# Grouped-query heads: softmax weights scaled on POOL ahead of their transposes, output kept feature-major

## The chip, the cores and the metric

The kernel runs on one core of one Trainium2 chip. The metric is device time in microseconds of one execution, lower is better. Engines: PE does the matrix products and the transposes, PEld loads its stationary operands, DVE (vector), ACT (scalar, activations) and POOL (the general engine) do the elementwise work, SP issues the DMAs. Each engine has its own queue and works through it in order.

## The reference

The reference is a two-layer encoder over 1024 tokens of 1024 features, in float32. The change lies in one part of the first layer, the grouped-query attention ("B" heads): 8 query heads of 64 features share 2 key/value heads.

```python
def gqa_attention(q, k, v):
    scale = HEAD_DIM ** -0.5
    def block(qb):                       # 128 queries at a time
        s = jnp.einsum('bqgrd,bkgd->bgrqk', qb, k).astype(jnp.float32) * scale
        pr = jax.nn.softmax(s, axis=-1).astype(v.dtype)
        return jnp.einsum('bgrqk,bkgd->bqgrd', pr, v)
    return from_blocks(lax.map(block, to_blocks(q)))
...
    b_o = gqa_attention(b_q, b_k, b_v)
    mix = jnp.concatenate([a_o.reshape(b, s, A_V), b_o.reshape(b, s, B_Q)], axis=-1)
    return mix @ w_out
```

The softmax divides by the sum of its row. Whether that is done to the weights ahead of the product with V, or to the product, is the same in exact arithmetic.

## The kernel before, in words

**Three-product precision.** A float32 operand of a matrix product is kept as two parts: `hi`, rounded to PE's fast format (fp32r), and `lo`, what is left. A product is then hi·hi + hi·lo + lo·hi. Making the parts costs one ACT instruction (`hi`, a rounding copy) and one DVE instruction (`lo`, a subtraction) each time. `H` is the operand of the projections: features in partitions, tokens along the free dimension ("feature-major").

**The even mixer** (method `even`) runs 96 items in one software pipeline, `its`: u = 0 to 3 are the differential heads (8 items each, one per block of 128 queries), u = 4 and 5 are the two key/value heads of the grouped-query part, with 32 items each: 8 query blocks `qt`, and 4 query heads j in each. So the grouped-query items are n = 32 to 95. The loop over n calls `step(n)`; a step works on several items at different ages, and this order, written out by hand, is also the order of each engine's queue:

- `qk(n)`: scores on PE (lines 964 and 969) into an `S` tile of PSUM (2 buffers), their negated maximum on DVE (line 972);
- `tr(n - 2)`: eight 128x128 transposes on PE (line 1007) of the weights `P`, into two `b` banks of PSUM (4 buffers, shared with everything else that PE writes), and the rounding copies to `pt` on ACT (line 1017);
- `exp(n)`: the exponential on ACT, 128x1024, with its row sum (line 981);
- `tr2(n - 2)`: the `lo` parts on DVE (line 1029);
- `combine(n)`: for odd j, the reciprocals of the two row sums of a pair of heads (line 996);
- `pv(n - 3)`: for odd j, the product of both heads' `pt` with V, 16 matmuls (line 1044). V's `hi` sits in output partitions 0 to 63 and its `lo` in 64 to 127, so the result has two halves that still have to be added;
- `tail_b(n - 4)`: for odd j, two transposes of 64 rows (line 1073), and the multiplication by the reciprocals on DVE (line 1078), into a token-major tile `MS`;
- `tail_a(n - 3)`: for odd j, the addition of the two halves: a copy on ACT (line 1061), an addition on DVE (line 1062);
- `place_b(n - 5)`: once per query block, two 128x128 transposes of `MS` (line 1090), and the parts for `H` (lines 1093 and 1094);
- `background(2)`: two pieces of the rotary work of the key/value head that comes next, on POOL (lines 834 to 850). The last batch, 18 pieces, is queued at n = 37 and taken at 37 to 45.

Between the halves of a step the loop puts other work for PE: a tile of the input projection at steps up to 37 (lines 175 to 177, 384 columns), the transposes of `finish(5)` at 49 to 60, `place_a` (the differential heads' output, line 1090 on `mix`) at the even steps 40 to 54, and a tile of the output projection (512 columns) at steps 57 to 63 by 2 and 67 to 100 by 3.

`own` in the code names the two halves of the partitions: `own[0]` is 0 to 63, `own[1]` is 64 to 127. `self.os()` gives a small SBUF tile of 128x256 (7 buffers), `self.tb()` a PSUM bank `b`, `self.col()` a few columns for per-row values.

Of the kernel before, what the change touches and what calls it, by code (L numbers as in the profile page):

```python
# [11 lines left out]
F32 = mybir.dt.float32  # L12
F32R = mybir.dt.float32r
AF = mybir.ActivationFunctionType
ALU = mybir.AluOpType
# [10 lines left out]
P = 128  # L26
# [80 lines left out]
class Kern:  # L107
# [657 lines left out]
    def even(self, W, ready, load, after):  # L765
        nc, a = self.nc, self.a
# [25 lines left out]
        own = (slice(0, 64), slice(64, 128))  # L792
# [155 lines left out]
        L, MS = {}, {}  # L948
# [35 lines left out]
        def combine(n):  # L984
            u, qt, j = its[n]
            e = L[n]
            if u < 4:
                r = e["r"] = self.col(3)
                s0 = e["s"][:, 0:1]
                nc.vector.reciprocal(r[:, 0:2], e["s"])  # L990
                nc.vector.scalar_tensor_tensor(r[:, 2:3], s0, nlam, r[:, 1:2], op0=ALU.mult, op1=ALU.mult)
                nc.vector.scalar_tensor_tensor(e["P"][0], e["P"][1], r[:, 2:3], e["P"][0],
                                               op0=ALU.mult, op1=ALU.add)
            elif j % 2 == 1:
                r = e["r"] = self.col(2)
                nc.vector.reciprocal(r, e["s"])

        def tr(n):
            u, qt, j = its[n]
# [49 lines left out]
        def tail_a(n):  # L1049
            u, qt, j = its[n]  # L1050
            e = L[n]
            if u < 4:
                os = e["os"] = self.os()
                ss = self.col()
                xo = M[u][:, qt, :]
                nc.scalar.activation(os[:, :P], e["o"][:, :P], AF.Copy, scale=e["r"][:, 0:1])
                nc.scalar.activation(xo, os[:, :P], AF.Square, accum_out=ss)
                e["rs"] = self.rstd(ss, 1.0 / P)
            elif j % 2 == 1:
                os = e["os"] = self.os()  # L1060
                nc.scalar.copy(os[0:64], e["o"][64:128, :256])
                nc.vector.tensor_add(os[0:64], e["o"][0:64, :256], os[0:64])

        def tail_b(n):
            u, qt, j = its[n]
            e = L[n]
            if u < 4:
                xo = M[u][:, qt, :]
                nc.vector.scalar_tensor_tensor(xo, e["os"][:, :P], e["rs"], gs, op0=ALU.mult, op1=ALU.mult)
            elif j % 2 == 1:  # L1070
                ps = self.tb()
                for b in range(2):
                    nc.tensor.transpose(ps[:, b * 64:b * 64 + 64], e["os"][0:64, b * P:(b + 1) * P],
                                        self.ident[0:64, 0:64])
                if j == 1:
                    MS[u, qt] = self.os()
                xo = MS[u, qt][:, (j // 2) * P:(j // 2 + 1) * P].rearrange("p (h d) -> p h d", h=2)
                nc.vector.tensor_mul(xo, ps[:, :P].rearrange("p (h d) -> p h d", h=2),
                                     e["r"][:, :, None].to_broadcast([P, 2, 64]))
            L.pop(n)  # L1080

        its = [(u, qt, j) for u in range(6) for qt in range(NT) for j in range(1 if u < 4 else 4)]
# [2 lines left out]
        def place(src, k0, t):  # L1085

            ps = self.tb()
            n = len(src)
            for k, x in enumerate(src):
                nc.tensor.transpose(ps[:, k * P:(k + 1) * P], x, self.ident)  # L1090
            v = ps[:, :n * P].rearrange("p (k c) -> p k c", k=n)
            h, l = self.hT2(slice(k0, k0 + n), slice(t * P, (t + 1) * P))
            nc.scalar.copy(h, v)
            nc.vector.tensor_sub(l, v, h.bitcast(F32))
# [6 lines left out]
        def place_b(n):  # L1101
            u, qt, j = its[n]
            ms = MS.pop((u, qt))
            place([ms[:, :P], ms[:, P:]], 2 * u - 4, qt)

        def step(n):

            A = lambda m: 0 <= m < 32
            B = lambda m: 32 <= m < N
            if n < N:  # L1110
                qk(n)
            if A(n - 2):
                pv(n - 2)
            if B(n - 2):
                tr(n - 2)
            if n < N:
                exp(n)
            if B(n - 2):
                tr2(n - 2)
            if A(n - 2):  # L1120
                tail_a(n - 2)
            if A(n - 4):
                tail_b(n - 4)
            yield
            if A(n - 1):
                tr(n - 1)
                tr2(n - 1)
            if n < N:
                combine(n)
            if B(n - 3):  # L1130
                pv(n - 3)
            if B(n - 4):
                tail_b(n - 4)
            if B(n - 3):
                tail_a(n - 3)
            if B(n - 5) and its[n - 5][2] == 3:
                place_b(n - 5)
            background(4 if n < 32 else 2)
            yield
# [35 lines left out]
        for n in range(N + 6):  # L1175
# [4 lines left out]
            s = step(n)  # L1180
# [511 lines left out]
```

## Time and profile before

| | |
|---|---|
| median of 3 runs | 2802.2 us (2801.87 to 2803.43) |
| the profiled execution | 2802.09 us, span 2800.0 us |
| PE busy | 2735.4 us, 98% of the span |
| PEld | 2265.7 us, 81% |
| DVE | 1920.9 us, 69% |
| ACT | 1402.5 us, 50% |
| POOL | 669.5 us, 24% |
| mean granted TensorE clock | 0.992 of full speed |
| grouped-query stage | about 384 to 658 us |

The span is the profiled stretch of that execution, from the first to the last instruction. The busy share of an engine is an average over stages with different limits; what a change in one stage is worth is read from that stage. Matmuls are pipelined, so rows of PE overlap: a row's duration is longer than what it adds, and the distance between the starts of neighbours tells more. In brackets behind a row of the timeline stands the time the engine was idle ahead of it, and which instruction ended that.

### The profile page before, as it was taken

The numbers are of one execution on the slowest core, as the hardware profiler recorded it, in microseconds if no ns is written. First come the engines' busy times: TensorE is split into PE (matmuls) and PEld (weight loads), VectorE is DVE, ScalarE is ACT, GpSimd is POOL, SyncE is SP. The second block draws the span as 40 slices with busy tenths as digits, with TensorE's granted clock in tenths as the row PEclk, the third lists the DMA queues.
The fourth block names the chain that finished last, engine by engine and source line by source line (L and its number), as shares of the span: only waits on it lengthen the run. The fifth ranks groups of instructions, "written<-read, shape, count | busy, mean of one in ns | idle before, by whom it ended". The sixth has DMA issues, their size and how long they took to land. (4 is left out here: it accounts for less than half of the span.)

```text
span 2800.0 us, 37183 instructions
## 1 busy us (share of the span) xinstructions
PE 2735.4 (98%) x13776; PEld 2265.7 (81%) x13776; DVE 1920.9 (69%) x3004; ACT 1402.5 (50%) x2727; POOL 669.5 (24%) x756
## 2 busy tenths in 40 slices
PE   8999999999899999999999999999989999999998
PEld 8988877777788888888887878877878888888887
DVE  5677778775677777677645666666667777777753
ACT  4455557563454444534523666666344444453532
POOL 2222751000544444100101001000244444400000
PEclk9999999999999999999999999999999999999999
DMA  4000001100134334833211111124023343472411
GB/s 161 1 24 24 27 8 46 46 16 33 46 135 151 122 126 150 287 119 123 92 68 71 37 58 49 38 71 160 16 97 120 138 151 136 169 274 84 147 46 60
DMA packets 101700, 260.77 MB, mean 93 GB/s; under 512 B 12048, under 2 KB 18320, under 8 KB 101520
## 3 DMA queue, kind: packets, MB, share of 16 engines
q1 hardware_dynamic: 101520, 258.40, 25.9%
q8 instruction: 109, 1.79, 0.3%
q14 instruction: 71, 0.58, 0.1%
HBM read 200.16 MB, written 58.20 MB: 92 GB/s over the span
## 5 line engine op out<-in xcount | busy, mean ns | idle before, releaser
L440 PE MATMUL b<-H,op 128*128 128x512 f32 x2016 | 484.2, 392 | 16.3 <-ACT op L323 13.2
L440 PEld LDWEIGHTS b<-H,op 128*128 128x128 f32 x2016 | 380.4, 189 | 97.0 <-ACT op L323 13.7
L440 PE MATMUL S<-T,op 128*128 128x512 f32 x1512 | 364.3, 390 | 2.2 <-DVE S L464 1.0
L175 PE MATMUL b<-hi,H 128*128 128x512 f32 (+1 forms) x896 | 337.5, 377 | 1.4 <-ACT H L1292 1.4
L440 PEld LDWEIGHTS S<-T,op 128*128 128x128 f32 x1512 | 283.0, 188 | 63.0 <-issue 2.1
L176 PE MATMUL b<-lo,H 128*128 128x512 f32 (+1 forms) x896 | 329.5, 368 | 1.1 <-DVE lo L165 1.1
L177 PE MATMUL b<-hi,H 128*128 128x512 f32 (+1 forms) x896 | 329.9, 368 | 0.4 <-DVE H L1293 0.4
L182 POOL TENSOR_SCALAR col<-col 128x1 f32<-128x1 f32 (+2 forms) x100 | 28.8, 288 | 1254.0 <-ACT xs L222 1072.9
L576 PE MATMUL S<-do,do 128*128 128x512 f32 x924 | 276.6, 390 | 3.5 <-ACT do L323 2.1
L576 PE MATMUL b<-do,do 128*128 128x512 f32 x924 | 275.5, 389 | 0.0
L576 PEld LDWEIGHTS S<-do,do 128*128 128x128 f32 x924 | 172.5, 188 | 41.8 <-ACT do L323 2.9
L576 PEld LDWEIGHTS b<-do,do 128*128 128x128 f32 x924 | 173.5, 188 | 36.2
L981 ACT ACTIVATE P<-S,col 128x1024 f32<-128x1024 f32 x128 | 143.2, 1119 | 111.4 <-DVE col L972 108.9
L324 DVE TENSOR_TENSOR op<-sm,op 128x512 fp32r<-128x512 f32 x168 | 133.2, 793 | 93.2 <-ACT op L323 93.0
L175 PEld LDWEIGHTS b<-hi,H 128*128 128x128 f32 x896 | 169.2, 189 | 22.8 <-ACT H L1292 1.8
L177 PEld LDWEIGHTS b<-hi,H 128*128 128x128 f32 x896 | 168.9, 189 | 21.7 <-DVE H L1293 1.1
L176 PEld LDWEIGHTS b<-lo,H 128*128 128x128 f32 x896 | 169.3, 189 | 21.0 <-DVE lo L165 2.5
L324 DVE TENSOR_TENSOR op<-raw,op 128x512 fp32r<-128x512 f32 x126 | 162.2, 1308 | 2.5 <-ACT op L323 2.1
L972 DVE TENSOR_REDUCE col<-S 128x1 f32<-128x1024 f32 x128 | 153.1, 1216 | 11.1 <-PE S L969 10.1
L175 PE MATMUL b<-H,hi 128*128 128x512 f32 x384 | 157.1, 409 | 0.2 <-ACT H L238 0.2
L177 PE MATMUL b<-H,lo 128*128 128x512 f32 x384 | 150.2, 391 | 0.0
L176 PE MATMUL b<-H,hi 128*128 128x512 f32 x384 | 149.9, 390 | 0.2 <-DVE H L239 0.2
(199 smaller groups left out, 5269.5 us busy)
## 6 DMA issues: line engine op xcount, KB each, us to landing
raw<-in_w_up SPq DMA_DIRECT2D x88, 512.0 KB, 4.8
g_dram<-cv SPq DMA_DIRECT2D x44, 512.0 KB, 2.6
we<-in_w_down SPq DMA_DIRECT2D x44, 512.0 KB, 4.9
wt_dram<-we SPq DMA_DIRECT2D x88, 256.0 KB, 3.1
wd<-wt_dram SPq DMA_DIRECT2D x88, 256.0 KB, 2.9
wd<-in_w_down SPq DMA_DIRECT2D x66, 256.0 KB, 5.3
G<-g_dram SPq DMA_DIRECT2D x64, 256.0 KB, 5.4
raw<-in_w_inc SPq DMA_DIRECT2D x24, 512.0 KB, 3.8
```

Source lines behind the costliest of these rows:

```text
L175: mm(out, st[0], mv[0], start=start, stop=False)
L176: mm(out, st[0], mv[1], start=False, stop=False)
L177: mm(out, st[1], mv[0], start=False, stop=stop)
L182: self.nc.gpsimd.tensor_scalar(r, ss, inv_n, EPS, op0=ALU.mult, op1=ALU.add)
L324: nc.vector.tensor_sub(o[:, 1], src, o[:, 0].bitcast(F32))
L440: mm(out, w[:, x, k], moving(n, y, k), start=(fresh and k + x + y == 0), stop=(k == 3 and x == 1), skip_group_check=True)
L576: mm(out[t], A[:, x, t * P:(t + 1) * P], B[:, y], start=(fresh and k == 0 and x + y == 0), stop=(k == NC - 1 and x == 1), skip_group_check ...
L972: nc.vector.tensor_reduce(nm, ps, axis=AX.X, op=ALU.max, negate=True)
L981: nc.scalar.activation(p, ps, AF.Exp, bias=nm, accum_out=e["s"][:, c:c + 1])
```

## The change

Three edits belong together, all for the grouped-query items alone.

1. In `combine(n)`, for every j, the reciprocal of this head's row sum is taken, and POOL multiplies the 128x1024 weights by it, in place. This stands ahead of the transposes of the same item, two steps later. Line 996 is now one column per head and step; line 997 is new.
2. In `tail_a`, the two halves are added so that the first head of the pair lands in partitions 0 to 63 of a tile and the second in 64 to 127: two copies of 64x128 on ACT (line 1066) and two additions on DVE (line 1068). Since the scale is already in, this is the operand's layout, features in partitions, and no transposes follow: the branch in `tail_b` goes.
3. `place_b` makes `hi` and `lo` from that tile directly (lines 1102 and 1103), without transposes. Both inputs of the subtraction are in SBUF.

```diff
@@ combine
-            elif j % 2 == 1:
-                r = e["r"] = self.col(2)
-                nc.vector.reciprocal(r, e["s"])
+            else:
+                r = self.col()
+                nc.vector.reciprocal(r, e["s"][:, j % 2:j % 2 + 1])
+                nc.gpsimd.tensor_scalar(e["P"][0], e["P"][0], r, None, op0=ALU.mult)
@@ tail_a
             elif j % 2 == 1:
-                os = e["os"] = self.os()
-                nc.scalar.copy(os[0:64], e["o"][64:128, :256])
-                nc.vector.tensor_add(os[0:64], e["o"][0:64, :256], os[0:64])
+                if j == 1:
+                    MS[u, qt] = self.os()
+                xo = MS[u, qt][:, (j // 2) * P:(j // 2 + 1) * P]
+                os, o = self.os(), e["o"]
+                for s in range(2):
+                    nc.scalar.copy(os[own[s], :P], o[own[1 - s], s * P:(s + 1) * P])
+                for s in range(2):
+                    nc.vector.tensor_add(xo[own[s]], o[own[s], s * P:(s + 1) * P], os[own[s], :P])
@@ tail_b
-            elif j % 2 == 1:
-                ps = self.tb()
-                for b in range(2):
-                    nc.tensor.transpose(ps[:, b * 64:b * 64 + 64], e["os"][0:64, b * P:(b + 1) * P],
-                                        self.ident[0:64, 0:64])
-                if j == 1:
-                    MS[u, qt] = self.os()
-                xo = MS[u, qt][:, (j // 2) * P:(j // 2 + 1) * P].rearrange("p (h d) -> p h d", h=2)
-                nc.vector.tensor_mul(xo, ps[:, :P].rearrange("p (h d) -> p h d", h=2),
-                                     e["r"][:, :, None].to_broadcast([P, 2, 64]))
@@ place_b
-            place([ms[:, :P], ms[:, P:]], 2 * u - 4, qt)
+            v = ms.rearrange("p (k c) -> p k c", k=2)
+            h, l = self.hT2(slice(2 * u - 4, 2 * u - 2), slice(qt * P, (qt + 1) * P))
+            nc.scalar.copy(h, v)
+            nc.vector.tensor_sub(l, v, h.bitcast(F32))
```

How this moves the queues is shown at three places. First PE, steps 41 and 42, before: `S` are scores, `P` weights, `os` the added halves of a pair, `b` a PSUM bank.

```order
L964 MATMUL S_4357<-ks_3730,qs_3600 128x512 x2
L969 MATMUL S_4357<-kl_3731,qs_3600 128x512 x2
L1007 MATMUL b_4364<-ident,P_4283 128x128 x4
L1007 MATMUL b_4369<-ident,P_4283 128x128 x4
L1073 MATMUL b_4382<-ident,os_4340 128x64 x2
L964 MATMUL S_4391<-ks_3730,qs_3861 128x512 x2
L969 MATMUL S_4391<-kl_3731,qs_3861 128x512 x2
```

The same steps of PE in the changed program:

```order
L964 MATMUL S_4372<-ks_3730,qs_3600 128x512 x2
L969 MATMUL S_4372<-kl_3731,qs_3600 128x512 x2
L1008 MATMUL b_4379<-ident,P_4298 128x128 x4
L1008 MATMUL b_4384<-ident,P_4298 128x128 x4
L964 MATMUL S_4402<-ks_3730,qs_3861 128x512 x2
L969 MATMUL S_4402<-kl_3731,qs_3861 128x512 x2
```

L1073 is gone, and with it a bank `b`; the transposes of `P` (now line 1008) read what POOL has written.

Second POOL, the rotary work of the last batch at steps 39 to 41, before: `T` are queries and keys, `gq` their gains, `rt` products with the sine table `tabB`.

```order
L834 TENSOR_TENSOR T_3269<-T_3269,col_4205 128x512
L834 TENSOR_TENSOR T_3270<-T_3270,col_4260 128x256
L837 TENSOR_TENSOR T_3268<-T_3268,gq 128x512
L837 TENSOR_TENSOR T_3269<-T_3269,gq 128x512
L837 TENSOR_TENSOR T_3270<-T_3270,gq 128x256
L841 TENSOR_TENSOR rt_4194<-T_3268,tabB_163 128x16x16
```

And in the changed program:

```order
L834 TENSOR_TENSOR T_3269<-T_3269,col_4215 128x512
L834 TENSOR_TENSOR T_3270<-T_3270,col_4275 128x256
L997 TENSOR_SCALAR P_4331<-P_4331,col_4335 128x1024
L837 TENSOR_TENSOR T_3268<-T_3268,gq 128x512
L837 TENSOR_TENSOR T_3269<-T_3269,gq 128x512
L997 TENSOR_SCALAR P_4391<-P_4391,col_4395 128x1024
L837 TENSOR_TENSOR T_3270<-T_3270,gq 128x256
L841 TENSOR_TENSOR rt_4204<-T_3268,tabB_163 128x16x16
```

A scaling of the weights now stands between every two pieces; each waits for its step's exponential, so the pieces behind it do too.

Third DVE, a step with P·V and `place_b` (n = 44) and the step behind it, before; `H` is the projection's operand, the second L1094 is `place_a`:

```order
L972 TENSOR_REDUCE col_4488<-S_4483 128x1
L1029 TENSOR_TENSOR pt_4501<-b_4490,pt_4500 128x4x128
L1029 TENSOR_TENSOR pt_4503<-b_4495,pt_4502 128x4x128
L1062 TENSOR_TENSOR os_4527<-b_4510,os_4527 64x256
L1094 TENSOR_TENSOR H_80<-b_4530,H_78 128x2x128
L1094 TENSOR_TENSOR H_79<-b_4539,H_77 128x4x128
L972 TENSOR_REDUCE col_4551<-S_4546 128x1
L1029 TENSOR_TENSOR pt_4501<-b_4553,pt_4500 128x4x128
L1029 TENSOR_TENSOR pt_4503<-b_4558,pt_4502 128x4x128
L996 RECIPROCAL col_4569<-col_4482 128x2
L1078 TENSOR_TENSOR os_4574<-b_4571,col_4380 128x128
```

And in the changed program:

```order
L1030 TENSOR_TENSOR pt_4514<-b_4503,pt_4513 128x4x128
L1030 TENSOR_TENSOR pt_4516<-b_4508,pt_4515 128x4x128
L996 RECIPROCAL col_4523<-col_4495 128x1
L1068 TENSOR_TENSOR os_4543<-b_4526,os_4544 64x128 x2
L1103 TENSOR_TENSOR H_80<-os_4355,H_78 128x2x128
L1090 TENSOR_TENSOR H_79<-b_4555,H_77 128x4x128
L972 TENSOR_REDUCE col_4567<-S_4562 128x1
L1030 TENSOR_TENSOR pt_4514<-b_4569,pt_4513 128x4x128
L1030 TENSOR_TENSOR pt_4516<-b_4574,pt_4515 128x4x128
L996 RECIPROCAL col_4585<-col_4495 128x1
```

A reciprocal stands in every step, ahead of the additions; L1078 is gone; L1103 reads the tile `os` where L1094 read the bank `b`.

## Rows read from the trace of the kernel before

**Rows 1.** Windows: busy us (count) of PE, PEld, DVE, ACT, POOL; clock; DMA; GB/s
```profile
403.00:475.00 72.00, 71.00 (x460) 53.63 (x460) 64.73 (x111) 56.03 (x107) 21.48 (x30) 1.00 0.11 38
475.00:658.00 183.00, 181.72 (x1080) 138.59 (x1079) 137.12 (x223) 108.02 (x204) 0.00 (x0) 1.00 0.10 33
```

**Rows 2.** Timeline of PE (start, us, engine, line), a step with L1073, then without
```profile
416.07 1.09 PE L1007 MATMUL b<-ident,P 128*128 128x128 f32 x8
417.36 0.74 PE L964 MATMUL S<-ks,qs 128*128 128x512 f32 x2
418.69 1.09 PE L1007 MATMUL b<-ident,P 128*128 128x128 f32 x8
419.54 2.16 PE L1044 MATMUL b<-pt,v 128*128 128x256 f32 x16
```

**Rows 3.** Timeline of PE, ends of projection tiles; P·V blocks without and with L1090
```profile
604.54 0.39 PE L177 MATMUL b<-hi,H 128*128 128x512 f32 x1
605.12 0.74 PE L964 MATMUL S<-ks,qs 128*128 128x512 f32 x2
...
564.16 0.39 PE L177 MATMUL b<-hi,H 128*128 128x512 f32 x1
564.39 2.08 PE L1044 MATMUL b<-pt,v 128*128 128x256 f32 x16
...
607.30 2.16 PE L1044 MATMUL b<-pt,v 128*128 128x256 f32 x16
609.29 0.63 PE L964 MATMUL S<-ks,qs 128*128 128x512 f32 x2
...
581.32 2.16 PE L1044 MATMUL b<-pt,v 128*128 128x256 f32 x16
583.45 0.71 PE L964 MATMUL S<-ks,qs 128*128 128x512 f32 x2
```

**Rows 4.** Waits of PE, 380 to 720 us: us in total, times, longest
```profile
PE b L1007 <- DVE pt L1029: 1.1, 2, 0.8
PE b L1073 <- DVE os L1062: 0.9, 1, 0.9
```

**Rows 5.** Timeline of DVE, 420 to 426 us, idle before and its releaser in brackets
```profile
423.93 0.69 DVE L1029 TENSOR_TENSOR pt<-b,pt 128x512 fp32r<-128x512 f32 x1 [2.77 <-POOL T L846]
```

**Rows 6.** Groups of DVE by form, 385 to 665 us: busy us, mean ns, idle before
```profile
L1062 DVE TENSOR_TENSOR os<-b,os 64x256 f32<-64x256 f32 x32 | 13.3, 416 | 20.9 <-ACT os L1061 20.7
L1078 DVE TENSOR_TENSOR os<-b,col 128x128 f32<-128x128 f32 x32 | 9.0, 282 | 0.4 <-PE b L1073 0.4
L996 DVE RECIPROCAL col<-col 128x2 f32<-128x2 f32 x32 | 5.2, 162 | 4.1 <-ACT P L981 3.0
```

**Rows 7.** Groups of POOL by form, 380 to 680 us
```profile
L834 POOL TENSOR_TENSOR T<-T,col 128x512 f32<-128x512 f32 x2 | 2.0, 1042 | 0.0
L837 POOL TENSOR_TENSOR T<-T,gq 128x512 f32<-128x512 f32 x2 | 2.5, 1286 | 0.0
```

**Rows 8.** Groups of POOL by form, whole span
```profile
L405 POOL TENSOR_TENSOR sm<-raw,sm 128x512 f32<-128x512 f32 x42 | 72.1, 1716 | 0.0
```

**Rows 9.** Timeline of ACT: the accumulator reads that end two exponentials
```profile
408.17 0.19 ACT L981 ACTIVATION_READ_ACCUMULATOR P<-S,col 128x1 f32 x1
...
571.65 0.19 ACT L981 ACTIVATION_READ_ACCUMULATOR P<-S,col 128x1 f32 x1
```

**Rows 10.** Timeline of PE: two groups of transposes L1007
```profile
441.59 1.09 PE L1007 MATMUL b<-ident,P 128*128 128x128 f32 x8
...
575.10 1.09 PE L1007 MATMUL b<-ident,P 128*128 128x128 f32 x8
```

**Rows 11.** Timeline of POOL, 404 to 428 us: one row of its rope work
```profile
407.79 1.64 POOL L183 TENSOR_TENSOR col<-col,mhalf 128x8 f32<-128x8 f32 x1
```

**Rows 12.** Groups of DVE by form, whole span
```profile
L324 DVE TENSOR_TENSOR op<-raw,op 128x512 fp32r<-128x512 f32 x126 | 162.2, 1308 | 2.5 <-ACT op L323 2.1
L324 DVE TENSOR_TENSOR do<-wd,do 128x512 fp32r<-128x512 f32 x154 | 105.6, 686 | 9.3 <-ACT do L323 9.3
```

## Prediction

> **What bounds the kernel now.** I read the windows first, with the edges set by the first and last grouped-query step. From 403 to 475 us PE is busy for 71.00 of 72.00 us, from 475 to 658 us for 181.72 of 183.00, at full granted clock in both; DVE is busy for 64.73 and 137.12, ACT for less [rows 1]. The reader is to see that PE sets the time in both stretches, with DVE close behind in the first (90%) and far behind in the second (75%). Then I read PE's timeline, from start to start, because the durations of its rows overlap: there the price of a PE instruction is what it puts between its neighbours. The waits of PE and the timeline of DVE came next, for the few holes in PE, and the groups of POOL and DVE by form last, for the prices of what is added. POOL works on the second KV head's rotary tables in the first stretch and has nothing to do in the second [rows 1].
>
> **PE: what goes.** 32 pairs of 64-row transposes (L1073) stand between other work of PE, one pair for two steps. Where one stands between the transposes L1007 and the next scores, 417.36 - 416.07 = 1.29 us pass; without it, from L1007 to P·V, 419.54 - 418.69 = 0.85 [rows 2]. It costs 0.44 us. Behind a tile of the projection the two gaps are 605.12 - 604.54 = 0.58 and 564.39 - 564.16 = 0.23, which makes 0.35 [rows 3]. The projection has a tile in 16 steps from 57 on (n is 57 to 63 by 2, 67 to 100 by 3); 10 of these are odd, and the pair stands in odd steps. So 22 x 0.44 + 10 x 0.35 = 13.2 us. The 16 pairs of 128-wide transposes in `place_b` (L1090 on `os`) widen the distance from P·V to the scores from 609.29 - 607.30 = 1.99 to 583.45 - 581.32 = 2.13 [rows 3]: 16 x 0.14 = 2.2 us. Two stalls go with them. The last L1073 waited 0.9 us for DVE's L1062. And one group of L1007 waited 0.8 us [rows 4] for a bank that DVE held while it stood 2.77 us for POOL [rows 5]: its next buffer came from the rotary tables, which POOL had not finished with; in the changed program that buffer goes to another tile, which needs it later. Sum: 13.2 + 2.2 + 0.9 + 0.8 = 17.1 us, all on the path, since PE is the bound.
>
> **DVE and ACT: what changes.** For each pair of heads DVE loses L1078 (0.28 us) and trades L1062 (0.42) for two additions of half the columns, and the one reciprocal (0.16) for two [rows 6]. A half addition is not in the trace; between half of L1062 (0.21) and the whole of it (0.42) I take 0.28, the price of L1078, which has as many columns. Per pair: 0.16 + 2 x 0.28 - 0.42 - 0.28 = +0.02 us, so nothing. That is hidden by PE as long as DVE has room. In the first stretch PE would need 72 us less ten pairs at 0.44, five `place_b` at 0.14 and the stall, 5.9 us: 66.1, against 64.7 of DVE. DVE also stands some 0.65 us per pair for ACT's copy behind P·V (20.9 us for 32) [rows 6], 6.5 us for ten pairs, and cannot have both. Between no loss and all of the 5.9 I take 2.5, since DVE's 2.77 us at POOL come free in this stretch. ACT trades a copy of 256 columns for two of 128; it is busy for 78% and 59% of the two stretches [rows 1], and the second copy runs beside the first addition.
>
> **POOL: what is added.** 64 multiplications of 128x1024 by one value per row, each ahead of the transposes of its block. The trace before has no such form. The nearest row is L834, which multiplies 512 columns by a value repeated along 64 of them: 1.04 us; L837, as long, but with a second operand that changes along the row, takes 1.29 [rows 7]. So it is the fetch of the second operand that is paid for, and the new form has no second operand of that kind. Its price S lies between 1.04 us (1024 columns at half of L834's price per column) and 3.43 (two of L405, 1.72 each, the dearest 512 columns on POOL) [rows 8]. I take 1.2, a little above the lower end: the row it is nearest to is L834, with half as much to fetch. The other readings are kept: 2.08 for two of L834, 2.57 for two of L837.
> The Trainium skill (GPSIMD Engine Reference, Engine selection) calls an elementwise operation with one input roughly line-rate; at the 1.2 GHz that the page gives, 1024 columns would be an estimated 0.85 us, no run here shows it, and the sum below would be the same by it.
>
> **POOL: is it in time?** PE's transposes of step n stand two steps behind the exponential of n, so PE has a cushion. The shortest that I found in mid-stage: the exponential's sum ends at 571.65 + 0.19 = 571.84, its transposes start at 575.10 [rows 9, 10]: 3.26 us. Less 0.5 for the faster PE, 0.16 for the reciprocal and 0.1 for two hand-overs, 2.5 us are left. S = 1.2 fits, 2.57 just about; 3.43 is 0.9 short. What stands behind PE's new wait is everything: P·V and the next scores are behind the transposes on PE.
> The tight place is the rotary stretch. There POOL's queue goes from "rope work as fast as it comes" to "one scaling, two pieces of rope work, one scaling, ...". Its 21.48 us between 403 and 475 [rows 1] begin with two pairs of small operations that end at 407.79 + 1.64 = 409.43 [rows 11]; two times 1.84 are 3.7, so 17.8 us are left. Between the scalings that follow step 38 (exponential ended at 408.36 [rows 9]) and step 46 (transposes at 441.59 [rows 10]) POOL has 9 S + 17.8 us to do. PE needs the last at 441.6 less four pairs at 0.58 and the stall of 0.8, so there are 438.5 - 409.4 = 29.1 us. S = 1.2 gives 28.6: no delay. S = 2.08 gives 36.5, 7.4 late, and every late microsecond is PE's.
>
> **`place_b` on SBUF.** Its subtraction took one operand from PSUM; now both are in SBUF. On this chip's FFN the same subtraction of 512 columns, both from SBUF, takes 0.69 us in one group and 1.31 in another [rows 12], and the dear ones stand where POOL works. 16 such subtractions may each meet a scaling. If all did, at 1.2 us, DVE would lose 19 us; if none, nothing. I take 1.0 us of it on PE's path, since a scaling runs for 1.2 of some 4 us and PE needs the result steps later.
> The Trainium skill (SBUF — State Buffer, Who interferes with whom) says that a DVE instruction with two SBUF inputs and a GpSimd instruction that reads SBUF exclude each other for a whole instruction. The FFN's 1.31 against 0.69 agrees; by that rule the sum would stay as it is, unless every meeting hit the path.
>
> **Sum.** -17.1 + 2.5 + 1.0 = -13.6 us. The profiled execution took 2802.09 us (span 2800.0), the median is 2802.2, so nothing is to be corrected: 2788.5 us. Its own range is 2785 (all 17.1) to 2791.
>
> **Rivals.**
> A, POOL is the bound in the rotary stretch. S = 2.08: 7.4 late, -6.2, 2796 us; S = 2.57: 9 x 2.57 + 17.8 = 40.9, 11.8 late, -1.8, 2800.5. For it: L834 is a real multiplication on this engine, and one cannot see in it what its second stream costs. Against: L837's extra 0.25 us.
> B, slower: the scaling does not end before PE wants it, all through the stage. S = 3.43: the rotary stretch is 9 x 3.43 + 17.8 - 29.1 = 19.6 late; in addition the cushion is 0.9 short in the 12 or so tight steps (one in three behind 475 us), 11 us, and some 0.3 in 14 steps ahead of that, 4 us. -13.6 + 34.6 = +21: 2823 us. It decides from S = 2.8 on, where the rotary stretch alone eats the gain. For it: L405's 1.72 us, when DVE competes. Against: in this stage DVE mostly reads PSUM with one operand, and L834 and L837 ran here without that surcharge.
> C, DVE takes over the first stretch fully: all 5.9 us of it are lost instead of 2.5, -10.2, 2792 us. For it: 90% busy. Against: its stall at POOL is gone, and there is one bank fewer to free per pair.
>
> **Chances.** Forecast 0.62, C 0.08, A with 2.08 0.17, A with 2.57 0.07, B 0.06. A measurement of this kernel tells a change from none at about 0.2%, 5.6 us. Faster by more: the forecast, C and two thirds of A at 2.08, 0.81. Within 0.2%: the rest of A, 0.13. Slower: B, 0.06. The range for 8 in 10 leaves out B and A at 2.57 and takes in A at 2.08: 2784.5 to 2797.5.
>
> **What would show it.** Right: L997 of about 1.0 to 1.4 us on POOL; from the transposes to the scores 0.85 us in every step; no wait of PE for POOL in front of the transposes between 404 and 440 us; the last P·V of the stage some 14 us earlier, and all behind it shifted as one. Wrong: PE rows that wait for POOL L997 (A in the rotary stretch, B throughout); DVE 97% busy from 403 to 470 with PE waiting for `pt` (C); an L1103 of a microsecond and more; or stages behind 665 us that change their own length.

## The result, and the profile after

The median of six runs is 2812.23 us (2810.7 to 2813.2) for the changed kernel against 2803.24 (2801.87 to 2804.03) for the one before, ratio 1.0034, 95% interval 1.0023 to 1.0045. The change makes the kernel slower by 9 us, where 13.6 us less were forecast; 2812 lies above the whole range. The profiled execution has a span of 2811.0 us, 11.0 more than before. All of it arises in the grouped-query stage: the last group of transposes of the stage starts at 662.72 us instead of 650.82, 11.9 later (start, us; in brackets the idle time ahead of it; before, then changed):
```profile
650.82 1.04 PE L1007 MATMUL b<-ident,P 128*128 128x128 f32 x8
662.72 1.09 PE L1008 MATMUL b<-ident,P 128*128 128x128 f32 x8 [1.79 <-POOL P L997]
```
In the changed kernel L964 and L969 are the scores, L1008 the transposes of `P`, L1030 the `lo` parts of `pt`, L1045 P·V, L1086 the transposes of `place_a`, L996 the reciprocal and L997 the scaling.

The group of the new instruction on POOL comes first (as [rows 7]: count, busy us, mean ns, idle before and its releasers, 380 to 680 us of the changed kernel):
```profile
L997 POOL TENSOR_SCALAR P<-P,col 128x1024 f32<-128x1024 f32 x63 | 179.5, 2853 | 73.9 <-DVE col L996 62.3 <-PE b L1045 4.6 <-PE b L1008 4.6
L834 POOL TENSOR_TENSOR T<-T,col 128x512 f32<-128x512 f32 x2 | 2.1, 1046 | 0.0
```
The reader is to see 2853 ns where 1200 were forecast, and that L834 has not changed (1046 against 1042): the engine is no slower, the new form is dear. The waits of PE, 380 to 720 us, answer to [rows 4] (us in total, times, longest):
```profile
PE b L1008 <- POOL P L997: 19.1, 12, 4.1
```
19.1 us of waiting for the scaling, in 12 places, have come in, 12.7 us of them in six places from 403 to 475 us; the wait of L1073 has gone with its line. The windows have the edges of [rows 1] (PE, PEld, DVE, ACT, POOL, granted clock, DMA share, GB/s):
```profile
403.00:475.00 72.00, 58.99 (x338) 47.29 (x337) 52.91 (x91) 44.29 (x90) 63.19 (x45) 0.88 0.09 30
475.00:658.00 183.00, 177.70 (x1053) 137.21 (x1053) 151.66 (x259) 119.53 (x240) 123.62 (x44) 0.99 0.10 32
```
In the rotary stretch PE has fallen from 71.00 to 58.99 us, DVE and ACT with it, and POOL stands at 63.19; and the granted clock is 0.88, where it was 1.00. Both show at one place of PE's timeline (start, us, engine, line; in brackets the idle time before and what ended it), which answers to [rows 2]:
```profile
408.01 1.09 PE L1008 MATMUL b<-ident,P 128*128 128x128 f32 x8
408.86 0.71 PE L964 MATMUL S<-ks,qs 128*128 128x512 f32 x2
409.50 0.73 PE L969 MATMUL S<-kl,qs 64*128 64x512 f32 x2
414.34 1.54 PE L1008 MATMUL b<-ident,P 128*128 128x128 f32 x8 [4.11 <-POOL P L997]
415.53 3.36 PE L1045 MATMUL b<-pt,v 128*128 128x256 f32 x16
418.72 0.60 PE L1086 MATMUL b<-ident,mix 128*128 128x128 f32 x4
```
From the transposes to the scores 408.86 - 408.01 = 0.85 us pass, as forecast. Then PE stands 4.11 us for L997, and the block P·V behind that takes 3.36 us, not 2.16. What POOL did meanwhile:
```profile
404.54 2.85 POOL L997 TENSOR_SCALAR P<-P,col 128x1024 f32<-128x1024 f32 x1 [4.45 <-DVE col L996]
407.47 0.20 POOL L182 TENSOR_SCALAR col<-col 128x8 f32<-128x8 f32 x1
407.75 1.68 POOL L183 TENSOR_TENSOR col<-col,mhalf 128x8 f32<-128x8 f32 x1
409.51 0.20 POOL L182 TENSOR_SCALAR col<-col 128x8 f32<-128x8 f32 x1
409.80 1.65 POOL L183 TENSOR_TENSOR col<-col,mhalf 128x8 f32<-128x8 f32 x1
411.43 2.85 POOL L997 TENSOR_SCALAR P<-P,col 128x1024 f32<-128x1024 f32 x1
```
No gap from 404.54 on: the scaling that PE wants stands behind two pairs of rotary work, and takes 2.85 us itself. The same in windows of 2 us, with the columns of the windows above:
```profile
414.00:416.00 2.00, 1.66 (x10) 1.66 (x11) 0.32 (x1) 0.62 (x2) 1.84 (x4) 0.71 0.01 4
416.00:418.00 2.00, 2.00 (x11) 2.00 (x11) 1.23 (x3) 1.66 (x3) 2.00 (x2) 0.50 0.00 0
418.00:420.00 2.00, 2.00 (x14) 1.63 (x13) 0.50 (x2) 1.04 (x4) 2.00 (x2) 0.94 0.00 0
```
Behind the wait PE runs at 0.50, the lower of its two levels (1.2 GHz), and two microseconds later it is back at the upper (2.4 GHz; 1.00 from 420 to 422 us). That happens five times between 403 and 475 us: five P·V blocks take 3.36, 3.67, 3.66, 3.20 and 3.31 us, 6.4 more than five of 2.16. A sixth time comes at 523 us, behind a wait of 1.75 us, where a projection tile takes 4.41 us from its start to the scores instead of 2.83.

### The profile page after: what moved, and what is told of

It reads as the page before. It is cut to its first block, busy times and chain, and to the rows that moved or that the text cites. A ratio compares the mean times of both kernels' runs of the same rounds, so it can differ in the third digit from the quotient of the medians.

```text
span 2811.0 us, 37285 instructions
## 1 busy us (share of the span) xinstructions
PE 2727.0 (97%) x13680; PEld 2264.7 (81%) x13680; DVE 1932.5 (69%) x3036; ACT 1410.6 (50%) x2759; POOL 852.8 (30%) x820
## 5 line engine op out<-in xcount | busy, mean ns | idle before, releaser
L440 PE MATMUL b<-H,op 128*128 128x512 f32 x2016 | 484.6, 393 | 16.3 <-ACT op L323 13.3
L997 POOL TENSOR_SCALAR P<-P,col 128x1024 f32<-128x1024 f32 x64 | 182.4, 2853 | 74.0 <-DVE col L996 62.3
L175 PE MATMUL b<-H,hi 128*128 128x512 f32 x384 | 157.1, 409 | 0.2 <-ACT H L238 0.2
L1299 POOL TENSOR_TENSOR b<-rb,mask 128x128 f32<-128x128 f32 x80 | 41.4, 554 | 362.8 <-PE b L1368 210.2
```

The costliest lines, as they stand in the source:

```text
L175: mm(out, st[0], mv[0], start=start, stop=False)
L440: mm(out, w[:, x, k], moving(n, y, k), start=(fresh and k + x + y == 0), stop=(k == 3 and x == 1), skip_group_check=True)
L997: nc.gpsimd.tensor_scalar(e["P"][0], e["P"][0], r, None, op0=ALU.mult)
L1299: nc.gpsimd.tensor_tensor(b2[:, e].rearrange("p (r c) -> p r c", r=16), rb[:, :, 8 * o:8 * o + 8], mask[:, e].rearrange("p (r c) -> p r c" ...
```

## The experiments

All times below are medians, beside the kernel before on the same chip in the same session (2801.97 to 2802.83 us there). T1 to T10 are the rival accounts that each expectation names; T1 is the one that I held. The first four ask whether the scaling's price is the whole loss.

**The changed kernel without the scaling.**
```
-                nc.gpsimd.tensor_scalar(e["P"][0], e["P"][0], r, None, op0=ALU.mult)
```


> The changed kernel without the scaling L997 on POOL; the output is left unscaled in the grouped-query heads, all else stands. Theory T1 (the price of the scaling, 2.85 us each, is the whole loss; the PE edits gain what was forecast): -17.1 + 2.5 for DVE, no contention of L1103 with POOL, 2788.6 us (2785 to 2793); no PE wait in front of L1008, granted clock 1.00 from 403 to 475 us, L1103 at 0.42 us. Rival T2 (the gain on PE is not there, or the split copies and the SBUF subtraction eat it): 2800 us or more with DVE or ACT in front of PE.

2787.69 us against 2802.61, ratio 0.9950 (0.9938 to 0.9963): -14.9, where T1 has -14.6. In the profiled execution, the slowest of the five (2790.71 us), the last transposes of the stage stand at 639.11 us, 11.7 ahead of the kernel before (650.82). The windows over the rotary stretch and over the rest of this shorter stage:
```profile
403.00:475.00 72.00, 69.01 (x437) 51.38 (x437) 66.43 (x120) 56.52 (x116) 21.70 (x30) 1.00 0.11 38
475.00:646.00 171.00, 169.99 (x1018) 133.30 (x1017) 139.67 (x244) 111.98 (x226) 0.00 (x0) 1.00 0.11 36
```
Clock 1.00, PE nearly full, DVE at 66.43 of 72: T2 falls. The gain of the PE edits is there, and the +9 of the changed kernel is 23.9 us of loss on top of it.

**The scaling alone, on the kernel before.**
```
-            elif j % 2 == 1:
-                r = e["r"] = self.col(2)
-                nc.vector.reciprocal(r, e["s"])
+            else:
+                r = e["r"] = self.col(2) if j % 2 == 0 else L[n - 1]["r"]
+                r = r[:, j % 2:j % 2 + 1]
+                nc.vector.reciprocal(r, e["s"][:, j % 2:j % 2 + 1])
+                nc.gpsimd.tensor_scalar(e["P"][0], e["P"][0], r, None, op0=ALU.mult)
```


> The kernel before, with one reciprocal and the POOL scaling added per step, nothing else changed; the tails still multiply, so these heads are scaled twice. T1: the rotary stretch has 9 x 2.85 + 17.8 = 43.5 us of POOL work against 441.6 - 409.4 = 32.2 us, 11.3 late, and PE runs at a lower granted clock behind its waits, some 5 us; behind 475 us the cushion of 3.26 us covers 2.85 + 0.16. 2819 us (2813 to 2824), more than the changed kernel. T2: the scaling is only a part of the +9 and the other edits cost the rest, so less than 2812.

2819.3 us against 2802.61, ratio 1.0059 (1.0046 to 1.0073): +16.7, T1's 2819; T2's "less than 2812" falls again. PE waits 12.7 us for the scaling, where the queue's account (9 S + 17.8 against what PE leaves) has 11.3; the rest is put down to the clock, 0.91 from 403 to 475 us. The two runs do not add up to the +9 (-14.9 + 16.7 = +1.8): in the changed kernel, with less work for PE, the same account leaves POOL 29.1 us instead of 32.2 and a cushion of 2.5 instead of 3.26.

**The scaling as a product of two tensors.**
```
-                nc.gpsimd.tensor_scalar(e["P"][0], e["P"][0], r, None, op0=ALU.mult)
+                nc.gpsimd.tensor_tensor(e["P"][0], e["P"][0], r.to_broadcast([P, S]), op=ALU.mult)
```


> The changed kernel with the scaling written as a multiplication of two tensors (the column repeated along the row, as L834 does it) instead of by a value per row. T1: the form sets the price; 2 x 1.03 = 2.06 us each. Rotary stretch 9 x 2.06 + 17.8 = 36.3 against 29.1, 7.2 late, and some 4 us of clock: 2800 us (2795 to 2803). Rival T3 (POOL pays per element of this tile, whatever the form): 2.85 us again and 2812.

2802.81 us, ratio 1.0004 (0.9995 to 1.0013). One takes 1.90 us; PE's waits for it are
```profile
PE b L1008 <- POOL P L997: 7.4, 5, 2.2
```
So T3 falls: the same product of the same tile is a microsecond cheaper in another form, and PE's waits for it go from 19.1 to 7.4 us. The time ends at the upper edge of T1's 2795 to 2803.

**Rotary work spread.** In this order part of the rotary work stands behind the transposes that read its tiles, so part of the queries is rotated only in part; sizes and counts are the same.
```
-            background(4 if n < 32 else 2)
+            background(4 if n < 32 else 2 if n < 37 else 1)
```


> The changed kernel with one piece of rotary work per step instead of two from step 37 on, so that it ends near step 54 instead of 45. T1: POOL still has 18 x 2.85 + 21.5 = 72.8 us to do in the 18 steps, for which PE needs some 63, so the loss is spread, not gone: 2808 us (2803 to 2812), the PE waits shorter but more of them. Rival T4 (the burst of two pieces between two scalings is the cause, 2.85 us alone would fit under each step): PE waits all but gone, 2792 us.

2809.8 us, ratio 1.0027 (1.0016 to 1.0037), inside T1's 2803 to 2812; waits for L997 are 13.5 us in 11 places. T4 falls: the burst is at most a part of the cause (19.1 us with it), POOL has too much to do in these steps. Another wait, 4.0 us for the spread rotary work itself (L931 for L850), has come in and is part of this time.

**Two-tensor form and spread rotary work, in the order in which the transposes want it.** (The first edit of the two above, the second, and the order of the pieces:)
```
-                    for fs in zip(*parts):
+                    for fs in zip(*parts) if t < 7 else (parts[0], parts[2], parts[1]):
```


> The changed kernel with the two-tensor form of the scaling (1.90 us each), one piece of rotary work per step from step 37 on, and the pieces of the second half in the order in which the transposes want them (first query pair, key, second query pair). Theory T1 (POOL is late only where its work exceeds what PE leaves it): 18 x 1.90 + 21.5 = 55.7 us in steps 37 to 54 against some 59 us of PE, so it fits by a little; 2792 us (2788 to 2797), under both kernels, PE waits for L997 below 3 us in all, granted clock near 1.00. Rival T5 (DVE and POOL on the same tiles slow each other, so that the scaling costs DVE time wherever it runs): 2800 us or more, with L996, L1030 or L1103 longer than without the scaling.

2799.28 us, ratio 0.9992 (0.9983 to 1.0001): above T1's 2788 to 2797 and just under T5's 2800, and T1's account does not explain it. L997's waits are down to 2.3 us, as it says; but DVE's subtraction at the ends of blocks, whose group here is
```profile
L1103 DVE TENSOR_TENSOR H<-os,H 128x256 fp32r<-128x256 f32 x15 | 19.4, 1296 | 0.5
```
took 0.43 us without the scaling, and PE's waits for `pt` (L1030) have grown from 3.6 to 6.3 us. That is T5's mechanism, some 13 us of DVE. How much of the 11.6 us over the unscaled kernel is its work, and how much the clock's (0.94 to 0.97 from 403 to 475), is not settled.

**The scaling on ACT.**
```
-                nc.gpsimd.tensor_scalar(e["P"][0], e["P"][0], r, None, op0=ALU.mult)
+                nc.scalar.activation(e["P"][0], e["P"][0], AF.Copy, scale=r)
```


> The changed kernel with the scaling on ACT (a copy with a scale per row, 128x1024 from SBUF; L222 of that form takes 1.06 us) instead of POOL. T1 (the engine must have room): ACT would be busy for 56 + 20 x 1.06 = 77 of the some 66 us that PE needs between steps 38 and 57, 11 late, and for 120 + 47 of 177 us behind it, which fits: 2788 + 11 + some 3 for the clock = 2802 us (2796 to 2808). Rival T6 (any engine that is not POOL hides it): 2788 us.

2844.99 us, ratio 1.0160 (1.0146 to 1.0174). T6 falls, but T1's 2802 is far off too. The size was near (1.15 us each for 1.06); what I left out, as far as the trace shows, is the place in the queue, seen in the group's idle time:
```profile
L997 ACT ACTIVATE P<-P,col 128x1024 f32<-128x1024 f32 x63 | 72.5, 1150 | 33.5 <-DVE col L996 33.5
```
ACT stands 33.5 us for the reciprocal on DVE, 0.5 us at each scaling, with the copies of `pt` queued behind it, and PE's waits fall on `pt` and `os` (22.6 and 10.8 us from 380 to 720). No run tests this account by itself.

**Prices of POOL's forms.** In steps 66 to 89 of the kernel before, where POOL has nothing to do, one further operation per step into a spare tile; two sets of eight. One line of each set:
```
+                    g.tensor_scalar(o, w, c, None, op0=ALU.mult)
+                    g.tensor_scalar(o, w, c, 0.0, op0=ALU.mult, op1=ALU.add)
```


> The kernel before with one further POOL operation per step from 66 to 89 into a tile that nobody reads, eight forms in turn, for their prices. T1 (the form sets the price): multiplication by a value per row 2.85 us for 1024 columns, half for 512; by a constant the same if both are one path, or 1 us if the fetch of the column is what costs; two tensors with a repeated column 1.90, half for 512; two full tensors 2.6 (L837's rate) ; a copy 0.9 to 1.9. T3 (1024 columns cost the same in any form): 2.85 in all six of that size.

> The kernel before with one further POOL operation per step from 66 to 89 into a tile that nobody reads, eight more forms in turn. T9 (an instruction with one operation per element is the slow one, whatever the operation and its scalar, and any second operation mends it): multiply by the column and add 0.0, and two multiplications by constants, 1.13 us for 1024 columns; one addition, one subtraction, one maximum with a constant, 2.8; two operations on 512 columns 0.6; one multiplication on 256 columns 0.8 to 0.95, on 128 columns 0.5 to 0.6. Rival T10 (it is the single multiplication alone that is slow): the single addition, subtraction and maximum 1.1 us.

The groups of the first set, in the order: by a column, by a constant, the tile by itself (two full operands), a repeated column, by a column on 512, by a column and then by 1.0, a repeated column on 512, a copy:
```profile
L1144 POOL TENSOR_SCALAR form<-P,col 128x1024 f32<-128x1024 f32 x3 | 8.6, 2850 | 100.4 <-ACT P L981 96.1 <-PE b L1044 4.3
L1146 POOL TENSOR_SCALAR form<-P 128x1024 f32<-128x1024 f32 x3 | 8.3, 2772 | 5.8 <-ACT P L981 5.8
L1150 POOL TENSOR_TENSOR form<-P 128x1024 f32<-128x1024 f32 x3 | 5.7, 1896 | 10.1 <-PE b L1007 5.6 <-ACT P L981 4.5
L1148 POOL TENSOR_TENSOR form<-P,col 128x1024 f32<-128x1024 f32 x3 | 5.7, 1896 | 3.3 <-ACT P L981 2.6 <-PE b L176 0.7
L1154 POOL TENSOR_SCALAR form<-P,col 128x512 f32<-128x512 f32 x3 | 4.7, 1567 | 10.8 <-ACT P L981 10.8
L1158 POOL TENSOR_SCALAR form<-P,col 128x1024 f32<-128x1024 f32 x3 | 3.4, 1126 | 12.0 <-ACT P L981 12.0
L1156 POOL TENSOR_TENSOR form<-P,col 128x512 f32<-128x512 f32 x3 | 3.1, 1042 | 6.4 <-PE b L1044 3.8 <-ACT P L981 2.6
L1152 POOL COPY form<-P 128x1024 f32<-128x1024 f32 x3 | 3.1, 1040 | 5.4 <-ACT P L981 5.4
```
Of the second set: one addition; by a column and add 0.0, two constants; by a column and 1.0 on 512 columns; by a column alone on 128:
```profile
L1147 POOL TENSOR_SCALAR form<-P 128x1024 f32<-128x1024 f32 x3 | 8.3, 2780 | 8.5 <-ACT P L981 6.1 <-PE b L176 2.4
...
L1143 POOL TENSOR_SCALAR form<-P,col 128x1024 f32<-128x1024 f32 x3 | 3.4, 1133 | 97.1 <-ACT P L981 94.3 <-PE b L1044 2.7
L1145 POOL TENSOR_SCALAR form<-P 128x1024 f32<-128x1024 f32 x3 | 3.1, 1048 | 11.0 <-ACT P L981 11.0
...
L1153 POOL TENSOR_SCALAR form<-P,col 128x512 f32<-128x512 f32 x3 | 2.1, 691 | 5.5 <-ACT P L981 5.5
L1155 POOL TENSOR_SCALAR form<-P,col 128x128 f32<-128x128 f32 x3 | 1.8, 608 | 9.1 <-PE b L1044 4.7 <-ACT P L981 4.4
```
T3 and T10 fall, T9 holds: 2.77 to 2.85 us with one operation per element, whichever it is (a maximum 2774 ns, a subtraction 2776), 1.05 to 1.13 with two, and the source of the scalar (column or constant) is worth 0.08. One expectation failed: two full operands were to take 2.6 us, at the rate of L837, and took 1896 ns, the same as a repeated column.

**Single waits of PE.**
```
-                nc.gpsimd.tensor_scalar(e["P"][0], e["P"][0], r, None, op0=ALU.mult)
+                for _ in range({50: 2, 66: 3, 82: 5}.get(n, 0)):
+                    nc.gpsimd.tensor_scalar(e["P"][0], e["P"][0], 1.0, None, op0=ALU.mult)
```


> The changed kernel without the scaling, except two, three and five multiplications by 1 in steps 50, 66 and 82, where POOL has nothing else: three single waits of PE of different length, with normal work between them; the output is left unscaled. T7 (the granted clock falls behind a wait of PE): waits of some 2.4, 5.3 and 11 us less the room of each step, behind the longer two a stretch with rows at half speed (P.V 3.4 to 4.3 us instead of 2.16) and a clock below 1.00, then 1.00 again; 2788 + waits + some 2 to 3 us for each fall. Rival T8 (the low clock in the rotary stretch is of another cause, for instance of POOL working, or comes by itself): 1.00 throughout.

One run, 2803.98 us. The first and the last of the three waits on PE's timeline, each with the P·V block behind it (lines are one higher here; the middle wait is 3.20 us):
```profile
456.37 1.53 PE L1009 MATMUL b<-ident,P 128*128 128x128 f32 x8 [1.93 <-POOL P L998]
457.55 3.37 PE L1046 MATMUL b<-pt,v 128*128 128x256 f32 x16
...
602.65 1.97 PE L1009 MATMUL b<-ident,P 128*128 128x128 f32 x8 [8.88 <-POOL P L998]
604.27 3.38 PE L1046 MATMUL b<-pt,v 128*128 128x256 f32 x16
```
T8 falls: 14.0 us of waits, and behind each, with POOL at rest, rows at the lower level: P·V 3.37, 3.66 and 3.38 us against 2.16, the transposes 1.53, 1.15 and 1.97 against 1.09, together 1.7, 1.6 and 2.1 us. The shortest wait, 1.93 us, brings on as much as the others; T7 had it only for the longer two. The kernel lost 16.3 us over the unscaled one, 3 less than waits and slow rows add up to; with one run here, and runs of the unscaled kernel 4 us apart, that difference is not resolved.

**The scaling with a second operation in the same instruction.**
```
-                nc.gpsimd.tensor_scalar(e["P"][0], e["P"][0], r, None, op0=ALU.mult)
+                nc.gpsimd.tensor_scalar(e["P"][0], e["P"][0], r, 1.0, op0=ALU.mult, op1=ALU.mult)
```


> The changed kernel, the scaling still a value-per-row multiplication on POOL, but with a second operation in the same instruction (times 1.0), which took 1.13 us for 128x1024 where the single one took 2.85. T1 (the size of S is the one term that failed): S = 1.13 is the forecast's 1.2, rotary stretch 9 x 1.13 + 17.8 = 28.0 against 29.1 us, no delay: 2789 us (2786 to 2793), no PE wait for L997 over 1 us, granted clock 1.00 in the rotary stretch. Rival T5 (the meeting of POOL's scaling with DVE's SBUF instructions costs the rest): 2794 to 2800 us, with L1103 near 0.8 us or more and PE behind pt.

2789.41 us against 2801.97, ratio 0.9954 (0.9942 to 0.9967): **-12.6 us, faster than both kernels.** Its rotary stretch, and what is left of PE's wait for L997 in the stage:
```profile
403.00:475.00 72.00, 67.97 (x434) 50.79 (x432) 66.24 (x117) 56.25 (x115) 43.19 (x49) 1.00 0.11 38
```
```profile
PE b L1008 <- POOL P L997: 1.0, 2, 0.6
```
Clock 1.00, POOL 43.19 instead of 63.19. T5 is bounded: L1103 has a mean of 0.56 us against 0.43, and the whole price over the unscaled kernel is 1.7 us, or 2.3 when each is taken against the kernel before of its own session (-12.6 and -14.9), within the spread of the two.

**The same with the rotary work spread.** With the edits of the spreading and the order, and
```
+                nc.gpsimd.tensor_scalar(e["P"][0], e["P"][0], r, 1.0, op0=ALU.mult, op1=ALU.mult)
```


> The same with one piece of rotary work per step from 37 on, in the order in which the transposes want them. T1: POOL has 18 x 1.13 + 21.5 = 41.8 us of work in steps 37 to 54 for some 59 us of PE: nothing is late, 2788.5 us (2786 to 2792), equal to the unscaled kernel's 2787.7 within a microsecond or two. T5: no better than without the spreading, 2794 us or more.

2789.85 us, ratio 0.9956 (0.9943 to 0.9970): as the last one. With 1.13 us per scaling there is nothing left to spread.

**The cheap scaling alone, on the kernel before.** The edit of the second experiment, but with
```
-                nc.gpsimd.tensor_scalar(e["P"][0], e["P"][0], r, None, op0=ALU.mult)
+                nc.gpsimd.tensor_scalar(e["P"][0], e["P"][0], r, 1.0, op0=ALU.mult, op1=ALU.mult)
```


> The kernel before with one reciprocal per step and the POOL scaling in its two-operation form added, nothing else; these heads are scaled twice. T1 (the scaling costs only what does not fit beside PE): rotary stretch 9 x 1.13 + 17.8 = 28.0 us against 32.2, cushion 3.26 against 1.13 + 0.16: nothing is late, 2802.5 us (2800 to 2805). Rival T5 (the scaling costs time by itself, at DVE or in SBUF): 2806 us or more.

2800.17 us against 2802.11, ratio 0.9992 (0.9983 to 1.0001), in T1's range; T5 falls here. At 2.85 us the same 64 instructions cost 16.7 us, at 1.13 nothing that could be measured.

## Why the prediction was wrong

**The step that failed** is the price of the scaling: "So it is the fetch of the second operand that is paid for, and the new form has no second operand of that kind ... I take 1.2". L997 takes 2.85 us. The row that it was read from, L834 in [rows 7], is another form of instruction, two tensors at 1.9 us per 1024 columns, and I went from it to a form of which the trace had no row, downward. The reason given did not hold either: it rests on L837's 1.29 us against L834's 1.04, and in the runs of the forms a second operand that changes along the row cost no more than a repeated one (1896 ns both). Why L837 takes longer is open. The right size was inside the bounds (1.04 to 3.43), just over rival B's "from S = 2.8 on", and B had 0.06; B's own 2823 was worked out for the upper end. A product with one tensor operand can be had at about the size taken: the two-operation form takes 1.13. The one-operation form, which the change uses, cannot.

**The account of POOL's queue** was right as a mechanism. With S = 2.85 it gives 9 x 2.85 + 17.8 - 29.1 = 14.4 us late in the rotary stretch and 0.35 us in some 12 steps behind it, 4 us: -13.6 + 18.6 = +5. Measured: +9.0. PE waits for L997 for 12.7 us in the rotary stretch, 0.6 to 4.1 us in each of six places, and for 5.4 us in five places later, 0.5 to 1.8 in each: near the account in their sums, but the later ones are fewer and longer than its 12 of 0.35.

**A term that was missing** is the clock: the forecast let PE lose only the time that it stands. Five P·V blocks at the lower level are 6.4 us, the transposes in front of them another 1.7, and the projection tile at 523 us 1.6; the single waits show that such rows follow from waits. Two windows, from 380 us to the last transposes of the stage, in the changed and in the unscaled kernel, show what of it lies on PE's path:
```profile
380.00:662.72 282.72, 261.45 (x1538) 205.74 (x1537) 223.10 (x384) 179.15 (x360) 208.08 (x106) 0.96 0.10 33
380.00:639.11 259.11, 255.11 (x1547) 198.59 (x1546) 217.04 (x383) 178.88 (x362) 27.35 (x41) 1.00 0.11 36
```
The scaling makes this stage 23.6 us longer. PE stands 21.3 us instead of 4.0, 17.3 more; the new waits are 19.1, but of 3.6 us of waits for `pt` only 1.7 are left. PE's busy time is 6.3 us longer; of the 9.7 of slow rows 3.4 are made up elsewhere, and where was not traced. Not every wait brings slow rows on. In the changed kernel 1.58 us at 424 did (P·V 3.67), but 1.79 at 662.72 did not (P·V 2.08), and with the rotary work spread 2.09 us at 412.65 did not (2.16). So the length of the wait alone does not decide it, and what does is open.

**PE: what goes** was right: 17.1 less 2.5 for DVE, 14.6 forecast, 14.9 measured without the scaling. In that kernel, behind 475 us, the distance from transposes to scores is 0.85 us; from P·V to the scores it is 1.99 to 2.02 in 14 places and 1.91 in the five behind a tile ([rows 3]: 2.13 with L1090); and from a tile to the scores it is 0.23, where it was 0.58.

**DVE and ACT.** A half addition takes 0.288 us (0.28 taken), a reciprocal 0.161. Rival C, DVE as the bound, did not come: 66.4 of 72 us without the scaling, and PE waits for `pt` for 3.6 us in the whole stage, against 1.3 before, close to the 2.5 taken.

**`place_b` on SBUF.** Dear meetings were forecast (1.0 us on the path); in the changed kernel L1103 has a mean of 0.72 us, up to 2.34, which makes 4 us of DVE in a stage where DVE had room. With the two-operation scaling all costs of POOL and DVE together are 1.7 to 2.3 us.

**The sum.** Put S back to the size taken and the sum stands: 2788.5 forecast, 2789.4 measured with L997 at 1.13. So -17.1 + 2.5 + 1.0 was sound as a sum, and one assumed duration turned a gain of 0.46% into a loss of 0.34%.

## What to carry to other kernels

An operation that the trace does not show in its very form has no price yet: bound it, ask which value turns the sign, and if that value lies inside the bounds, measure it in a stretch where its engine is idle before anything is built on it; and try another form of the same arithmetic. Where an engine joins the chain in front of PE, add up its work in the stretch where it was busy already, not over the stage. A wait in front of a full PE can cost more than its length, since PE may go on at half its clock behind it: 1.9 us of waiting brought on another 1.7 in one run, while 1.8 us elsewhere brought on none. Look at the rows behind each wait.

## What the runs showed of the hardware

POOL's instruction that combines a tile with a scalar (a column or a constant) has two speeds. With one operation it took 608, 1567 and 2850 ns for 128, 512 and 1024 columns, 2.5 ns per column; with two operations 691 and 1126 ns for 512 and 1024, 0.85 ns per column, a copy 1040 for 1024. The Trainium skill (GPSIMD Engine Reference, Engine selection) calls an elementwise operation with one input roughly line-rate. At the 1.2 GHz that the page gives, an estimated 0.83 ns per column, the two-operation form and the copy agree; the one-operation form does not, by a factor of three. Why a second operation makes the instruction shorter is open.

DVE's subtraction of two SBUF tiles (L1103) meets the forms differently. In each pair of rows below the scaling on POOL comes first: two tensors (the run with that form); one operation, where L1103 starts early and where it starts later (the changed kernel); two operations (the run with a second operation).
```profile
467.41 1.90 POOL L997 TENSOR_TENSOR P<-P,col 128x1024 f32<-128x1024 f32 x1 [2.61 <-DVE col L996]
467.92 1.67 DVE L1103 TENSOR_TENSOR H<-os,H 128x256 fp32r<-128x256 f32 x1
```
```profile
477.94 2.85 POOL L997 TENSOR_SCALAR P<-P,col 128x1024 f32<-128x1024 f32 x1 [1.66 <-DVE col L996]
478.43 0.90 DVE L1103 TENSOR_TENSOR H<-os,H 128x256 fp32r<-128x256 f32 x1
...
532.94 2.85 POOL L997 TENSOR_SCALAR P<-P,col 128x1024 f32<-128x1024 f32 x1 [0.54 <-DVE col L996]
533.93 0.42 DVE L1103 TENSOR_TENSOR H<-os,H 128x256 fp32r<-128x256 f32 x1
```
```profile
460.20 1.12 POOL L997 TENSOR_SCALAR P<-P,col 128x1024 f32<-128x1024 f32 x1 [3.38 <-DVE col L996]
460.69 0.91 DVE L1103 TENSOR_TENSOR H<-os,H 128x256 fp32r<-128x256 f32 x1
```
Against the two-tensor form L1103 ends 0.28 us behind it (469.59 and 469.31). Against the one-operation form it ends 1.39 us behind its start (479.33 - 477.94), and one that starts 0.99 behind it runs at full speed, with nearly 2 us of L997 to come; against the two-operation form it ends 1.40 behind the start (461.60 - 460.20). The other meetings in these runs agree: where the two-operation form or the one-operation form stood alone in the way and L1103 started within 1.01 us of it, L1103 ended 1.38 to 1.44 us behind its start. So both scalar forms hold DVE off for equally long, and the longer one has no part in that for the rest of its time. The Trainium skill (SBUF — State Buffer, SBUF: two separate sides) says that a DVE instruction with two SBUF inputs and a GpSimd instruction that reads SBUF exclude each other for a whole instruction: the two-tensor and the two-operation form agree, the one-operation form is left free for more than half of its time.
